# HGRN2 decay-weighted score blocks that grow by a factor of four instead of two

## The chip, the cores and the metric

The kernel runs on one core of one Trainium2 chip. The metric is the device time of one execution in microseconds; the figure for a kernel is the median of its runs. A profile is one further execution, recorded instruction by instruction.

## What is computed

One decoder layer is run for 320 tokens: 256 of one new prompt, and 8 tokens of each of 8 running sequences. An input projection feeds two token mixers, an mLSTM (branch A) and an HGRN2 recurrence (branch B); the branches are projected, gated and merged, and two LayerNorms and a feed-forward block follow. The change lies in branch B. Per head (8 heads, 128 key channels, 256 value channels) it computes

```
G = cumsum(log f)                                   # over the tokens, per channel
a[t,s] = sum_k q[t,k] * exp(G[t,k] - G[s,k]) * (1-f)[s,k]     for s <= t, else 0
o = a @ i + (q * exp(G)) @ S_0
S_new = exp(G_end) * S_0 + ((1-f) * exp(G_end - G))^T @ i
```

Because the decay depends on the channel, `a` isn't one matrix product. It is one product per block pair, once queries carry the decay from their block's start and keys the decay to their block's end.

## The kernel before

**The stream of weights.** All large products have weights as the stationary operand and the 320 tokens as the moving one. There are 304 tiles of 128 output channels; each has 16 contraction steps, and each step three matmuls of 320 columns (high part by high part, high by low, low by high: `bank<-xh,wh`, `xl,wh`, `xh,wl` and the like in the profile), so 304 x 16 x 3 = 14,592 matmuls, in `run_main`. Half a tile is a **unit**: 1,024 weights per partition, 24 matmuls. A unit's weights are fetched by SyncE into one of three buffers `wr`, split by ScalarE (`wh`, line 321) and VectorE (`wl = wr - wh`, line 469, in `prep`) into one of three pairs of buffers, and the pair is free again when its unit's matmuls are done.

**Side work.** Everything else (evacuations, the mixers) is written as Python generators, "chains", that a planner (`Sched`, `pump`) merges into the stream when the program is built. The planner holds a modelled clock for each engine and puts a side operation in when its inputs should be ready by that clock; a TensorE side operation is placed only when its inputs are at least 0.45 us old by the model. What it yields is a fixed order on each of the in-order queues of PE, DVE, ACT, POOL and SP; at run time only semaphores hold an instruction. Side matmuls on f32 data are recorded as two matmul records each.

**Branch B's chains.** A head has six tiles in the stream (two gate tiles, `hf`, `hq` and two of `hi`). From `hf` come the forget gates `fs[:,1]` and the keys `qk[:,0]`; `qk[:,1]` are the queries; `fs[:,0]` starts at one. `h_scan` (VectorE) then goes through block sizes B = 1, 2, 4, ..., 64 (`LEVELS`) and 128. At each size it

- writes `y` (line 1274): in one operation, left halves of each pair of blocks become keys times decay to the block's end, right halves queries times decay from the block's start;
- joins the blocks to blocks of 2B: the left half of `fs[:,0]` is multiplied by the right block's total (line 1279), the right half of `fs[:,1]` by the left one's (line 1281).

`h_a` follows it. For each size from 2 to 64 and each of the three 128-token tiles (two from size 8 on, where the 8-token sequences need no more) TensorE multiplies the tile of `y` as stationary operand with that tile's 64 right-half columns (`self.mm` in line 327), and VectorE copies what belongs to the block pairs into the score matrix `at` under a mask (line 1325). That is 2 x 3 + 4 x 2 = 14 products of 64 columns in a head. Size 1 goes by element products and a sum over channels with ones as weights; size 128 is one product of 128 columns. `y` for sizes from 2 up lies in a pool `yb` of two buffers. `h_state`, `h_i`, `h_out` and `h_sp` take it from there; they don't change.

Of the kernel before, what the change touches and what calls it, by code (L numbers as in the profile page):

```python
# [26 lines left out]
ALPHA = 2.0 ** 0.25  # L27
LEVELS = (1, 2, 4, 8, 16, 32, 64)

# [43 lines left out]

C_ID, C_TRI, C_BM, C_SEL, C_SC, C_END = 0, 128, 256, 320, 328, 968


def constants():
    c = np.zeros((128, C_END), np.float32)
    i = np.arange(128)
    c[:, C_ID:C_ID + 128] = i[:, None] == i[None, :]  # L80
    c[:, C_TRI:C_TRI + 128] = i[:, None] <= i[None, :]

    s = np.arange(64)
    t = s.reshape(2, 4, 8).transpose(1, 0, 2).reshape(64)
    c[64:, C_BM:C_BM + 64] = (s[:, None] <= t[None, :]) & (s[:, None] // 8 == t[None, :] // 8)
    for r in range(4):
        c[r, C_SEL + r] = c[r + 8, C_SEL + r] = 1.0
        c[r + 4, C_SEL + 4 + r] = c[r + 12, C_SEL + 4 + r] = 1.0
    start = np.zeros(TOK, bool)
    start[0] = True  # L90
    start[NP_::NT] = True
    c[:4, C_SC:C_SC + TOK] = ~start
    c[:4, C_SC + TOK:C_SC + 2 * TOK] = np.where(start, -1e38, 0.0)
    m = np.zeros((128, len(LEVELS), 64), np.int32)
    for n, b in enumerate(LEVELS):
        right = (i // b) % 2 == 1
        t = i[right]
        m[:, n, :] = (i[:, None] // (2 * b) == t[None, :] // (2 * b)) & ((i[:, None] // b) % 2 == 0)

    r = np.zeros((2, 64, 2, 4, 4, 8), np.float32)  # L100
    for b in range(NB):
        for n in range(4):
            for i in range(8):
                r[1 - n // 2, 8 * b + i, b // 4, b % 4, n, i] = 1.0
    return c, m.reshape(128, -1), r.reshape(128, 256)

# [120 lines left out]
def acq(pool, n=1):  # L227
    return ("acq", pool, n)
# [55 lines left out]
class Program:  # L284
    def __init__(self, tc, nc, d, pools):
        self.nc, self.d, self.s = nc, d, Sched()
        p, ps, self.dr = pools
        self.cst = p.tile([128, C_END], F32, name="cst")
        self.lmask = p.tile([128, len(LEVELS) * 64], U8, name="lmask")
        self.vec = p.tile([128, V_END], F32, name="vec")  # L290
# [42 lines left out]
    def carve(self):  # L333
# [42 lines left out]
        self.at = Pool([A(512) for _ in range(2)])  # L376
        self.yb = Pool([A(384) for _ in range(2)])
        self.ktk = Pool([A.three(2, 128)])
        self.it2 = [B.three(3, 256) for _ in range(2)]
# [21 lines left out]
    def carve_h(self):  # L401
# [4 lines left out]
        self.pp = Pool([pp])  # L406
        for x in (qz, self.ats0, pp[:, 480:512], *(y[64:128, 2, :] for y in self.it2)):
            self.nc.gpsimd.memset(x, 0.0)
# [180 lines left out]
    def start(self):  # L589
# [21 lines left out]
        self.dma(self.vec, d["vec"])  # L611
        self.dma(self.cst, d["cst"])
        lm = self.f2[:, 0:448].bitcast(I32)
        self.dma(lm, d["lmask"])
        self.dma(self.f2[:, 448:704], d["spread"])
        self.spread = self.ra[:, 6400:6656].rearrange("p (g n) -> p g n", g=2)
        nc.gpsimd.tensor_copy(self.lmask, lm)
        nc.gpsimd.tensor_copy(self.spread, self.f2[:, 448:704].rearrange("p (g n) -> p g n", g=2))
        nc.gpsimd.memset(self.ones_r.bitcast(F32), 1.0)
# [82 lines left out]
    def rows(self, b):  # L702
# [8 lines left out]
        m0 = row(8)  # L711
        emg = row(128)
        sel = self.cst[0:16, C_SEL:C_SEL + 8]
        yield ("sp", 620, lambda: self.dma(m0, self.d["m0"]))
        yield ("pool", 100, lambda: nc.gpsimd.memset(emg, 1.0))
        yield ("act", act(T, True), lambda: self.A(gs, b[0:16, :T]))
# [17 lines left out]
        yield ("dve", dve(T), lambda: v.scalar_tensor_tensor(lf, fx, 0.0, lnu, ALU.min, ALU.subtract))  # L734
        keep = self.cst[0:4, C_SC:C_SC + T]
        low = self.cst[0:4, C_SC + T:C_SC + 2 * T]
        yield ("dve", 2 * dve(T), lambda: v.tensor_tensor_scan(bb, keep, lf, 0.0, ALU.mult, ALU.add))
        yield ("dve", dve(T), lambda: v.tensor_tensor(a, ig, bb, ALU.subtract))
# [445 lines left out]
    def h_start(self, h):  # L1184
# [7 lines left out]
        m["i"] = [Ev(), Ev()]  # L1192
        m["Y"] = [Ev() for _ in range(9)]
        s = self.s
# [58 lines left out]
    def h_scan(self, h):  # L1253

        v, m = self.nc.vector, self.hh[h]
        yield wait(m["f"], m["q"], m["got"])
        qk, fs = m["qk"], m["fs"]
        m["y"] = [None] * 9
        for n, B in enumerate(LEVELS + (128,)):
            T = TOK if B < 8 else NP_  # L1260
            y = yield acq(self.yb if B > 1 else self.pp)
            pat = [[2 * B, T // (2 * B)], [320 + B, 2], [1, B]]
            patq = [[2 * B, T // (2 * B)], [384 + B, 2], [1, B]]
            if B == 1:

                yield ("dve", dve(T), lambda: v.tensor_tensor(y[:, 0:T], qk[:, 0, 0:T], qk[:, 1, 0:T], ALU.mult))
                yo, odd = y[:, T:T + T // 2], lambda x: x[:, 1, 1:T:2]
                yield ("dve", dve(T / 2), lambda: v.tensor_tensor(yo, qk[:, 0, 0:T:2], odd(qk), ALU.mult))
                yield ("dve", dve(T / 2), lambda: v.tensor_tensor(yo, yo, odd(fs), ALU.mult))
            else:  # L1270
                if B < 8:
                    yield ("pool", 150, lambda: self.nc.gpsimd.memset(y[:, 320:384], 0.0))
                yo = y[:, 0:T].rearrange("p (j c i) -> p j c i", c=2, i=B)
                yield ("dve", dve(T), lambda: v.tensor_tensor(yo, cap(qk, 0, patq), cap(fs, 0, pat), ALU.mult))
            m["y"][n] = y
            yield post(m["Y"][n])
            half = lambda x, r: cap(fs, 320 * x + B * r, [[2 * B, T // (2 * B)], [1, B]])
            tot = lambda r: cap(fs, 320 + B * r + B - 1, [[2 * B, T // (2 * B)], [0, B]])
            yield ("dve", dve(T / 2), lambda: v.tensor_tensor(half(0, 0), half(0, 0), tot(1), ALU.mult))
            if B < 128:  # L1280
                yield ("dve", dve(T / 2), lambda: v.tensor_tensor(half(1, 1), half(1, 1), tot(0), ALU.mult))
            if B == 4:
                yield post(m["pre8"])
            if B == 128:

                yield post(m["suf"])

    def h_a(self, h):
# [10 lines left out]
        idb = self.ident.unsqueeze(1).to_broadcast([128, 3, 128])  # L1299
        for n, B in enumerate(LEVELS):  # L1300
            yield wait(m["Y"][n])
            y = m["y"][n]
            w = 3 if B < 8 else 2
            if B == 1:
                hl = yield acq(self.phl)
                yield ("act", act(512), lambda: self.A(hl[0], y))
                yield ("dve", dve(512), lambda: v.tensor_tensor(hl[1], y, hl[0].bitcast(F32), ALU.subtract))
                yield rel(self.pp, y)
            b = yield acq(self.sbank)
            bv = b[:, 0:64 * w]  # L1310
            if B == 1:
                yield ("pe", 2 * pe_r(512), lambda: [self.mm(b, self.ones_r, x, start=i == 0, stop=i == 1) for i, x in enumerate(hl)])
                yield rel(self.phl, hl)
                yield ("dve", dve(384, True), lambda: v.tensor_tensor(a3, b[:, 0:384].rearrange("p (a t) -> p a t", a=3), idb, ALU.mult))
                bv = b[:, TOK:TOK + 192]
            else:
                for i in range(w):
                    c = slice(128 * i, 128 * i + 128)
                    right = y[:, c].rearrange("p (j c i) -> p j c i", c=2, i=B)[:, :, 1, :]
                    yield ("pe", pe_f(64), lambda: self.mm(b[:, 64 * i:64 * i + 64], y[:, c], right, start=True, stop=True))  # L1320
                yield rel(self.yb, y)
            ar = a3[:, 0:w, :].rearrange("p a (j c i) -> p a j c i", c=2, i=B)[:, :, :, 1, :]
            mk = self.lmask[:, 64 * n:64 * n + 64].unsqueeze(1).to_broadcast([128, w, 64]).rearrange("p a (j i) -> p a j i", i=B)
            bv = bv.rearrange("p (a j i) -> p a j i", a=w, i=B)
            yield ("dve", dve(64 * w, True) + (150 if w > 2 else 0), lambda: v.copy_predicated(ar, mk, bv))
            yield rel(self.sbank, b)
        yield wait(m["Y"][7])
        y = m["y"][7]
        b = yield acq(self.sbank)
# [517 lines left out]
    xT=(128, KT, TOK), wif=(128, KT, 8), wt=(len(UNITS), 128, 1024), vec=(128, V_END), m0=(MH, NB), n0=(128, 64),  # L1847
    C0=(MH, NB, 128, 1024), S0=(HH, 128, NB, HV), cst=(128, C_END), lmask=(128, len(LEVELS) * 64), spread=(128, 256),
)
# [70 lines left out]
```

## Time and profile before

| | us |
|---|---|
| median of 3 runs | 2336.71 (2336.39 to 2338.29) |
| the profiled execution | 2337.24 |
| its span, first to last instruction | 2335.5 |
| TensorE (PE) busy | 2320.3 |
| VectorE (DVE) busy | 1370.3 |
| ScalarE (ACT) busy | 1049.6 |
| GpSimd (POOL) busy | 13.4 |

The profile's page gives busy times of each engine, the span in 40 slices, the chain of work that ended last, and groups of instructions by line with the mean length of one. Lengths of TensorE records overlap: a matmul's record lasts until its last result is out, while the next one has long started, so that what a matmul costs the stream is read from the distances between starts. The timeline view lists instructions by their start, and joins neighbours of one kind into a row with their count (`x2`); an f32 product appears as such a row. The waits views tell what an engine's idle time ended with.

### The profile page before, as it was taken

Reading aid. Unit: us, or ns where it says so; the run is one execution under the profiler, and the core shown is the slowest. Engines: PE = TensorE matmul, PEld = TensorE weight load, DVE = VectorE, ACT = ScalarE, POOL = GpSimd, SP = SyncE. Lnnn points to the kernel's source line nnn. Section 1 sums busy time; section 2 is a strip of 40 time slices with the busy share of each in tenths; the row PEclk is TensorE's granted clock in tenths of the full one; section 3 lists DMA queues with packets and bytes.
Section 4 is the critical chain, followed back from the end, with each engine's and each line's share of the span. In section 5 each row is a group of like instructions: output and inputs, shape, how many; then the busy total and the mean of one; then the engine's idle time right before and its main releaser. Section 6 shows DMA issues by size and latency. Waiting matters only on the chain.

```text
span 2335.5 us, 39111 instructions
## 1 busy us (share of the span) xinstructions
PE 2320.3 (99%) x15858; PEld 2274.2 (97%) x15858; DVE 1370.3 (59%) x2320; ACT 1049.6 (45%) x1669; POOL 13.4 (1%) x57
## 2 busy tenths in 40 slices
PE   8999999999999999999999999999999999999998
PEld 7999999999999999999999999999999999999998
DVE  5566557666766776555555767544554455445555
ACT  4444445455555465444433446532443344334434
POOL 0000000000000000000000000000000000000000
PEclk9999999999999999999999999999999999999999
DMA  5777776555555554554555644444444444444465
GB/s 207 258 269 265 256 237 227 196 183 181 181 181 175 183 195 166 181 173 170 176 171 176 221 167 142 147 153 145 149 149 151 148 147 152 150 148 146 153 226 180
DMA packets 143564, 425.03 MB, mean 182 GB/s; under 512 B 16404, under 2 KB 37780, under 8 KB 142360
## 3 DMA queue, kind: packets, MB, share of 16 engines
q1 hardware_dynamic: 142232, 416.25, 51.7%
q0 software_dynamic: 1152, 6.29, 0.8%
q8 instruction: 124, 2.03, 0.4%
q14 instruction: 56, 0.46, 0.1%
HBM read 371.57 MB, written 50.90 MB: 181 GB/s over the span
## 4 chain that ended last, share of the span: by engine, by line
PE 98%; DVE 1%; DMA 0%; ACT 0%; SPq 0%; issue 0%; DVEq 0%
PE bank L327 97%; DVE f3m L1809 0%; DVE f3m L1814 0%; DMA wr<-wt 0%; PE bank L1113 0%; PE bank L1518 0%; PE bank L887 0%; DMA f<-scr 0%; PE bank L1348 0%; SPq L330 0%; PE bank L960 0%; PE bank L1406 0%; PE bank L1353 0%; PE bank L1467 0%; PE bank L934 0%
## 5 line engine op out<-in xcount | busy, mean ns | idle before, releaser
L469 DVE TENSOR_TENSOR wl<-wr,wh 128x1024 fp32r<-128x1024 f32 (+1 forms) x430 | 525.8, 1223 | 474.2 <-ACT wh L321 468.7
L327 PE MATMUL bank<-xh,wh 128*128 128x320 f32 (+1 forms) x2432 | 793.2, 326 | 0.7 <-ACT wh L321 0.7
L327 PE MATMUL bank<-xh,wl 128*128 128x320 f32 (+1 forms) x2432 | 754.0, 310 | 0.0
L327 PE MATMUL bank<-xl,wh 128*128 128x320 f32 (+1 forms) x2432 | 752.0, 309 | 0.0
L321 ACT ACTIVATE wh<-wr 128x1024 fp32r<-128x1024 f32 (+1 forms) x430 | 453.6, 1055 | 448.0 <-PE bank L327 426.1
L327 PEld LDWEIGHTS bank<-xh,wh 128*128 128x128 f32 x2432 | 459.0, 189 | 21.1 <-issue 15.0
L327 PEld LDWEIGHTS bank<-xl,wh 128*128 128x128 f32 x2432 | 459.6, 189 | 3.7
L327 PEld LDWEIGHTS bank<-xh,wl 128*128 128x128 f32 x2432 | 458.4, 188 | 0.2 <-DVE wl L469 0.2
L469 DVE TENSOR_TENSOR bb<-wr,bb 128x1024 fp32r<-128x1024 f32 x179 | 219.3, 1225 | 234.6 <-ACT bb L321 234.5
L327 PE MATMUL bank<-xh,bb 128*128 128x322 f32 x1280 | 287.2, 311 | 0.0
L327 PE MATMUL bank<-ra,bb 128*128 128x320 f32 x1264 | 283.6, 309 | 0.0
L321 ACT ACTIVATE bb<-wr 128x1024 fp32r<-128x1024 f32 x179 | 188.8, 1055 | 207.5 <-PE bank L327 199.8
L327 PE MATMUL bank<-rxb,bb 128*128 128x320 f32 x1112 | 255.4, 309 | 0.0
L327 PE MATMUL bank<-ra,wh 128*128 128x320 f32 x892 | 249.9, 309 | 0.0
L327 PEld LDWEIGHTS bank<-xh,bb 128*128 128x128 f32 x1280 | 215.9, 188 | 0.0
L327 PEld LDWEIGHTS bank<-ra,bb 128*128 128x128 f32 x1264 | 210.7, 188 | 0.4
L327 PE MATMUL bank<-xl,bb 128*128 128x322 f32 x640 | 198.7, 310 | 0.0
L327 PEld LDWEIGHTS bank<-rxb,bb 128*128 128x128 f32 x1112 | 188.4, 188 | 0.2
L321 ACT ACTIVATE f<-f,misc 128x320 f32<-128x320 f32 x210 | 118.2, 563 | 149.5 <-DVE f L1777 137.1
L327 PE MATMUL bank<-rxb,wh 128*128 128x320 f32 x596 | 184.2, 309 | 0.0
L327 PE MATMUL bank<-rxb,wl 128*128 128x320 f32 x596 | 183.8, 308 | 0.0
L327 PEld LDWEIGHTS bank<-ra,wh 128*128 128x128 f32 x892 | 161.5, 188 | 1.1 <-DVE ra L1548 0.9
(257 smaller groups left out, 2230.6 us busy)
## 6 DMA issues: line engine op xcount, KB each, us to landing
wr<-wt SPq DMA_DIRECT2D x607, 512.0 KB, 3.3
rx<-C SPq DMA_DIRECT2D x34, 256.0 KB, 5.7
Cs<-rx SPq DMA_DIRECT2D x34, 256.0 KB, 5.0
f<-C SPq DMA_DIRECT2D x30, 256.0 KB, 4.9
Cs<-f SPq DMA_DIRECT2D x30, 256.0 KB, 4.2
vD<-ra SPq DMA_DIRECT2D x4, 1024.0 KB, 7.1
f<-S SPq DMA_DIRECT2D x8, 512.0 KB, 6.1
f3h<-S SPq DMA_DIRECT2D x8, 512.0 KB, 5.7
```

Source lines behind the costliest of these rows:

```text
L321: return self.nc.scalar.activation(out, in_, func, **kw)
L327: self.nc.tensor.matmul(*a, **kw)
L469: self.V().tensor_tensor(lo[:, c], raw[:, c], hi[:, c].bitcast(F32), ALU.subtract)
```

## The change

Sizes now grow by four: after size 1 come 2, 8 and 32 (`QUADS`), and 128 as before. At each of these sizes four neighbouring blocks are handled together.

- `h_scan` writes into one buffer of 1,024 columns per partition: the keys of all tokens (columns 0 to 319), and from column 384 on, for each group of four blocks, the six (query block, distance) sets: blocks 1, 2, 3 at distance one, 2 and 3 at distance two, 3 at distance three. This takes four VectorE operations (T, 0.75 T, 0.5 T and 0.25 T columns, T being 320 or 256) where two sizes took two of T columns. The two joins to 2B and 4B follow one another. Size 128 is written by two operations of 128 columns.
- `h_a` multiplies each tile's keys once with all its query sets: 192 columns (96 for the third tile, of which half is used), 3 + 2 + 2 = 7 products in a head. Three masked copies per size, one per distance, take the results to `at`: nine in a head beside that of size 1, where there were six.
- `yb` has one buffer instead of two. The buffer of `ktk` moves to the space of `f3h`. The zeros behind the third tile's tokens are set once, and not by GpSimd for each size.
- Nine masks and that of size 1 take 928 columns instead of 448. To make room, `cst` keeps 328 of its 968 columns; the two rows of 320 that the mLSTM's scans read are fetched by two small DMAs into scratch in `rows`.

The diff, without the declarations of sizes:

```diff
-LEVELS = (1, 2, 4, 8, 16, 32, 64)
+QUADS = (2, 8, 32)
+C_KEPT = C_SC
+N_MASK = 64 + 480 + 2 * 192
...
-        self.yb = Pool([A(384) for _ in range(2)])
-        self.ktk = Pool([A.three(2, 128)])
+        self.yb0 = A(1024)
+        self.yb = Pool([self.yb0])
...
+        self.ktk = Pool([C.three(2, 128)])
-        for x in (qz, self.ats0, pp[:, 480:512], *(y[64:128, 2, :] for y in self.it2)):
+        for x in (qz, self.ats0, pp[:, 480:512], self.yb0[:, 320:384], *(y[64:128, 2, :] for y in self.it2)):
...
-        self.dma(self.cst, d["cst"])
-        lm = self.f2[:, 0:448].bitcast(I32)
+        self.dma(self.cst, d["cst"][:, 0:C_KEPT])
+        lm = self.f2[:, 0:N_MASK].bitcast(I32)
...
+        for n, x in enumerate((keep, low)):
+            sc = yield ("sp", 620, lambda: self.dma(x, self.d["cst"][0:4, C_SC + T * n:C_SC + T * n + T]))
...
-        yield ("dve", 2 * dve(T), lambda: v.tensor_tensor_scan(bb, keep, lf, 0.0, ALU.mult, ALU.add))
+        yield ("dve", 2 * dve(T), lambda: v.tensor_tensor_scan(bb, keep, lf, 0.0, ALU.mult, ALU.add), (sc + 3000.0,))
...
+        for n, B in enumerate(QUADS):
+            T = TOK if B == 2 else NP_
+            J = T // (4 * B)
+            z = y = m["y"][n + 1] = yield acq(self.yb)
+            q = lambda o, k: cap(z, 384 + B * o, [[6 * B, J], [B, k], [1, B]])
+            f = lambda o, k: cap(fs, 320 + B * o + B - 1, [[4 * B, J], [B, k], [0, B]])
+            yield ("dve", dve(T), lambda: v.tensor_tensor(z[:, 0:T], qk[:, 0, 0:T], fs[:, 0, 0:T], ALU.mult))
+            run = lambda x, o: cap(x, o + B, [[4 * B, J], [1, 3 * B]])
+            yield ("dve", dve(0.75 * T), lambda: v.tensor_tensor(cap(z, 384, [[6 * B, J], [1, 3 * B]]), run(qk, 384), run(fs, 320), ALU.mult))
+            yield ("dve", dve(T / 2), lambda: v.tensor_tensor(q(3, 2), q(1, 2), f(1, 2), ALU.mult))
+            yield ("dve", dve(T / 4), lambda: v.tensor_tensor(q(5, 1), q(4, 1), f(1, 1), ALU.mult))
+            yield post(m["Y"][n + 1])
+            yield from join(B, T)
+            yield from join(2 * B, T)
...
-                for i in range(w):
-                    c = slice(128 * i, 128 * i + 128)
-                    right = y[:, c].rearrange("p (j c i) -> p j c i", c=2, i=B)[:, :, 1, :]
-                    yield ("pe", pe_f(64), lambda: self.mm(b[:, 64 * i:64 * i + 64], y[:, c], right, start=True, stop=True))
+            for i in range(w):
+                k = 192 if i < 2 else 96
+                yield ("pe", pe_f(k), lambda: self.mm(b[:, 192 * i:192 * i + k], y[:, 128 * i:128 * i + 128], y[:, 384 + 192 * i:384 + 192 * i + k], start=True, stop=True))
+            yield rel(self.yb, y)
+            for d in (1, 2, 3):
+                k, o = (4 - d) * B, (0, 3, 5)[d - 1] * B
+                if B == 2:
+                    J, mk = 40, cap(self.lmask, at_mask, [[k, 40], [1, k]])
+                    to, of = cap(at, d * B, [[4 * B, J], [1, k]]), cap(b, o, [[6 * B, J], [1, k]])
+                    at_mask += 40 * k
+                else:
+                    mk = cap(self.lmask, at_mask, [[0, 2], [k, g], [1, k]])
+                    to, of = cap(at, d * B, [[128, 2], [4 * B, g], [1, k]]), cap(b, o, [[192, 2], [6 * B, g], [1, k]])
+                    at_mask += g * k
+                yield ("dve", dve(w * 32 * (4 - d), True), lambda: v.copy_predicated(to, mk, of))
```

More of the change, by code (lines that the diff above doesn't have):

```diff
@@ L93, in constants @@
     c[:4, C_SC + TOK:C_SC + 2 * TOK] = np.where(start, -1e38, 0.0)
[L94 to L98, printed above, removed]
+    t = i[1::2]
+    m = [i[:, None] == t[None, :] - 1]
+    for b in QUADS:
+        t = np.arange(TOK if b == 2 else 128)
+        own = (t // b) % 4
+        for d in (1, 2, 3):
+            u = t[own >= d] % 128
+            m.append((i[:, None] // (4 * b) == u[None, :] // (4 * b)) & ((i[:, None] // b) % 4 == (u[None, :] // b) % 4 - d))
+    m = np.concatenate(m, axis=1).astype(np.int32)
+    assert m.shape[1] == N_MASK
     r = np.zeros((2, 64, 2, 4, 4, 8), np.float32)
@@ L104, in constants @@
                 r[1 - n // 2, 8 * b + i, b // 4, b % 4, n, i] = 1.0
-    return c, m.reshape(128, -1), r.reshape(128, 256)
+    return c, m, r.reshape(128, 256)
 V_MLG, V_HGG, V_G1, V_B1, V_G2, V_B2, V_LB, V_BI, V_BF, V_END = 0, 16, 32, 48, 64, 80, 96, 112, 113, 114
@@ L287, in __init__ @@
         p, ps, self.dr = pools
-        self.cst = p.tile([128, C_END], F32, name="cst")
-        self.lmask = p.tile([128, len(LEVELS) * 64], U8, name="lmask")
+        self.cst = p.tile([128, C_KEPT], F32, name="cst")
+        self.lmask = p.tile([128, N_MASK], U8, name="lmask")
         self.vec = p.tile([128, V_END], F32, name="vec")
@@ L611, in start @@
         self.dma(self.vec, d["vec"])
-        self.dma(self.cst, d["cst"])
-        lm = self.f2[:, 0:448].bitcast(I32)
+        self.dma(self.cst, d["cst"][:, 0:C_KEPT])
+        lm = self.f2[:, 0:N_MASK].bitcast(I32)
         self.dma(lm, d["lmask"])
-        self.dma(self.f2[:, 448:704], d["spread"])
+        self.dma(self.f2[:, N_MASK:N_MASK + 256], d["spread"])
         self.spread = self.ra[:, 6400:6656].rearrange("p (g n) -> p g n", g=2)
         nc.gpsimd.tensor_copy(self.lmask, lm)
-        nc.gpsimd.tensor_copy(self.spread, self.f2[:, 448:704].rearrange("p (g n) -> p g n", g=2))
+        nc.gpsimd.tensor_copy(self.spread, self.f2[:, N_MASK:N_MASK + 256].rearrange("p (g n) -> p g n", g=2))
         nc.gpsimd.memset(self.ones_r.bitcast(F32), 1.0)
@@ L712, in rows @@
         emg = row(128)
+        keep, low = row(), row()
         sel = self.cst[0:16, C_SEL:C_SEL + 8]
         yield ("sp", 620, lambda: self.dma(m0, self.d["m0"]))
+        for n, x in enumerate((keep, low)):
+            sc = yield ("sp", 620, lambda: self.dma(x, self.d["cst"][0:4, C_SC + T * n:C_SC + T * n + T]))
         yield ("pool", 100, lambda: nc.gpsimd.memset(emg, 1.0))
@@ L734, in rows @@
         yield ("dve", dve(T), lambda: v.scalar_tensor_tensor(lf, fx, 0.0, lnu, ALU.min, ALU.subtract))
-        keep = self.cst[0:4, C_SC:C_SC + T]
-        low = self.cst[0:4, C_SC + T:C_SC + 2 * T]
-        yield ("dve", 2 * dve(T), lambda: v.tensor_tensor_scan(bb, keep, lf, 0.0, ALU.mult, ALU.add))
+        yield ("dve", 2 * dve(T), lambda: v.tensor_tensor_scan(bb, keep, lf, 0.0, ALU.mult, ALU.add), (sc + 3000.0,))
         yield ("dve", dve(T), lambda: v.tensor_tensor(a, ig, bb, ALU.subtract))
@@ L1192, in h_start @@
         m["i"] = [Ev(), Ev()]
-        m["Y"] = [Ev() for _ in range(9)]
+        m["Y"] = [Ev() for _ in range(5)]
         s = self.s
@@ L1257, in h_scan @@
         qk, fs = m["qk"], m["fs"]
[L1258 to L1279, printed above, removed]
-            if B < 128:
-                yield ("dve", dve(T / 2), lambda: v.tensor_tensor(half(1, 1), half(1, 1), tot(0), ALU.mult))
-            if B == 4:
-                yield post(m["pre8"])
-            if B == 128:
-                yield post(m["suf"])
@@ new lines, in h_scan, with join @@
+        m["y"] = [None] * 5
+        half = lambda x, r, B, T: cap(fs, 320 * x + B * r, [[2 * B, T // (2 * B)], [1, B]])
+        tot = lambda r, B, T: cap(fs, 320 + B * r + B - 1, [[2 * B, T // (2 * B)], [0, B]])
+        def join(B, T):
+            yield ("dve", dve(T / 2), lambda: v.tensor_tensor(half(0, 0, B, T), half(0, 0, B, T), tot(1, B, T), ALU.mult))
+            if B < 128:
+                yield ("dve", dve(T / 2), lambda: v.tensor_tensor(half(1, 1, B, T), half(1, 1, B, T), tot(0, B, T), ALU.mult))
@@ new lines, in h_scan @@
+        T = TOK
+        y = m["y"][0] = yield acq(self.pp)
+        yield ("dve", dve(T), lambda: v.tensor_tensor(y[:, 0:T], qk[:, 0, 0:T], qk[:, 1, 0:T], ALU.mult))
+        yo, odd = y[:, T:T + T // 2], lambda x: x[:, 1, 1:T:2]
+        yield ("dve", dve(T / 2), lambda: v.tensor_tensor(yo, qk[:, 0, 0:T:2], odd(qk), ALU.mult))
+        yield ("dve", dve(T / 2), lambda: v.tensor_tensor(yo, yo, odd(fs), ALU.mult))
+        yield post(m["Y"][0])
+        yield from join(1, T)
+        for n, B in enumerate(QUADS):
[13 more added lines that the diff above has]
+            if B == 2:
+                yield post(m["pre8"])
@@ L1288, in h_a @@
+        y = m["y"][4] = yield acq(self.yb)
+        for i in range(2):
+            yield ("dve", dve(128), lambda: v.tensor_tensor(y[:, 128 * i:128 * i + 128], qk[:, i, 128 * i:128 * i + 128], fs[:, i, 128 * i:128 * i + 128], ALU.mult))
+        yield post(m["Y"][4])
+        yield from join(128, NP_)
+        yield post(m["suf"])
     def h_a(self, h):
@@ L1299, in h_a @@
         idb = self.ident.unsqueeze(1).to_broadcast([128, 3, 128])
[L1300 to L1308, printed above, removed]
-            b = yield acq(self.sbank)
[L1310 to L1316, printed above, removed]
-                for i in range(w):
-                    c = slice(128 * i, 128 * i + 128)
-                    right = y[:, c].rearrange("p (j c i) -> p j c i", c=2, i=B)[:, :, 1, :]
-                    yield ("pe", pe_f(64), lambda: self.mm(b[:, 64 * i:64 * i + 64], y[:, c], right, start=True, stop=True))
[L1321 to L1325, printed above, removed]
@@ new lines, in h_a @@
+        yield wait(m["Y"][0])
+        y = m["y"][0]
+        hl = yield acq(self.phl)
+        yield ("act", act(512), lambda: self.A(hl[0], y))
+        yield ("dve", dve(512), lambda: v.tensor_tensor(hl[1], y, hl[0].bitcast(F32), ALU.subtract))
+        yield rel(self.pp, y)
+        b = yield acq(self.sbank)
+        yield ("pe", 2 * pe_r(512), lambda: [self.mm(b, self.ones_r, x, start=i == 0, stop=i == 1) for i, x in enumerate(hl)])
+        yield rel(self.phl, hl)
+        yield ("dve", dve(384, True), lambda: v.tensor_tensor(a3, b[:, 0:384].rearrange("p (a t) -> p a t", a=3), idb, ALU.mult))
@@ new lines, in h_a @@
+        mk = self.lmask[:, 0:64].unsqueeze(1).to_broadcast([128, 3, 64])
+        yield ("dve", dve(192, True) + 150, lambda: v.copy_predicated(a3[:, :, 1:128:2], mk, b[:, TOK:TOK + 192].rearrange("p (a t) -> p a t", a=3)))
+        yield rel(self.sbank, b)
+        at_mask = 64
+        for n, B in enumerate(QUADS):
+            yield wait(m["Y"][n + 1])
+            y = m["y"][n + 1]
+            b = yield acq(self.sbank)
+            w, g = (3 if B == 2 else 2), 128 // (4 * B)
+            for i in range(w):
+                k = 192 if i < 2 else 96
+                yield ("pe", pe_f(k), lambda: self.mm(b[:, 192 * i:192 * i + k], y[:, 128 * i:128 * i + 128], y[:, 384 + 192 * i:384 + 192 * i + k], start=True, stop=True))
+            yield rel(self.yb, y)
+            for d in (1, 2, 3):
+                k, o = (4 - d) * B, (0, 3, 5)[d - 1] * B
+                if B == 2:
+                    J, mk = 40, cap(self.lmask, at_mask, [[k, 40], [1, k]])
[6 more added lines that the diff above has]
+                yield ("dve", dve(w * 32 * (4 - d), True), lambda: v.copy_predicated(to, mk, of))
@@ L1326, in h_a @@
             yield rel(self.sbank, b)
-        yield wait(m["Y"][7])
-        y = m["y"][7]
+        yield wait(m["Y"][4])
+        y = m["y"][4]
         b = yield acq(self.sbank)
@@ L1847 @@
     xT=(128, KT, TOK), wif=(128, KT, 8), wt=(len(UNITS), 128, 1024), vec=(128, V_END), m0=(MH, NB), n0=(128, 64),
-    C0=(MH, NB, 128, 1024), S0=(HH, 128, NB, HV), cst=(128, C_END), lmask=(128, len(LEVELS) * 64), spread=(128, 256),
+    C0=(MH, NB, 128, 1024), S0=(HH, 128, NB, HV), cst=(128, C_END), lmask=(128, N_MASK), spread=(128, 256),
 )
```

## The prediction

> **What bounds the kernel now.** I read the page first, for the span and the busy times, then the table of stretches, then the chain of work that ended last.
>
> ```profile
> span 2335.5 us, 39111 instructions
> PE 2320.3 (99%) x15858; PEld 2274.2 (97%) x15858; DVE 1370.3 (59%) x2320; ACT 1049.6 (45%) x1669; POOL 13.4 (1%) x57
> PE 98%; DVE 1%; DMA 0%; ACT 0%; SPq 0%; issue 0%; DVEq 0%
> ```
>
> ```profile
> 0.00:30.00 30.00, 21.97 (x123) 17.32 (x124) 15.19 (x24) 14.29 (x20) 2.98 (x16) 1.00 0.73 262
> 30.00:2300.00 2270.00, 2269.50 (x15592) 2231.87 (x15591) 1336.24 (x2251) 1018.62 (x1615) 9.89 (x40) 1.00 0.52 180
> 2300.00:2336.00 36.00, 28.80 (x148) 25.03 (x147) 18.85 (x46) 16.74 (x34) 0.53 (x1) 0.94 0.68 247
> ```
>
> ```profile
> 440.00:830.00 390.00, 390.00 (x2806) 378.29 (x2804) 275.33 (x675) 201.03 (x404) 4.07 (x23) 1.00 0.53 181
> ```
>
> Behind a stretch stand its length and the busy time of PE, PEld (TensorE's loads of the stationary operand), DVE, ACT and POOL, then the granted clock. Between 30 and 2300 us TensorE is idle for 0.5 us; from 440 to 830 us, where branch B's scores are made, for nothing, at the full clock. A busy record alone wouldn't prove that the array is kept at its pace, since records overlap; the chain does:
>
> ```profile
> 862.57 1448.69 PE bank L327 x9823
> ```
>
> From 863 us on, 9,823 matmuls follow one another at 1448.69 / 9823 = 0.1475 us, nearly all of them the stream's 320-column ones. So TensorE is the bound; what the change takes out of its queue between 440 and 830 us the end gains, unless TensorE has to wait for something new. ScalarE, VectorE and GpSimd are covered as long as it doesn't.
>
> **What a score product costs the stream.** In the timeline of TensorE a row shows the start. I take the start of the last stream matmul ahead of a product and that of the second one behind it, and subtract two steps of the stream, 0.295 us.
>
> ```profile
> 442.89 0.31 PE L327 MATMUL bank<-xh,wl 128*128 128x320 f32 x1
> 443.04 0.33 PE L327 MATMUL bank<-f 128*128 128x64 f32 x2
> 443.18 0.39 PE L327 MATMUL bank<-xh,wh 128*128 128x320 f32 x1
> 443.41 0.30 PE L327 MATMUL bank<-xl,wh 128*128 128x320 f32 x1
> ```
>
> ```profile
> 773.47 0.31 PE L327 MATMUL bank<-xh,wl 128*128 128x320 f32 x1
> 773.62 0.38 PE L327 MATMUL bank<-f 128*128 128x128 f32 x2
> ...
> 773.99 0.30 PE L327 MATMUL bank<-xl,wh 128*128 128x320 f32 x1
> ```
>
> ```profile
> 776.54 0.31 PE L327 MATMUL bank<-xh,wl 128*128 128x320 f32 x1
> 776.69 0.59 PE L327 MATMUL bank<-f,f 128*128 128x256 f32 x2
> ...
> 777.27 0.31 PE L327 MATMUL bank<-xl,wh 128*128 128x320 f32 x1
> ```
>
> ```profile
> 2304.07 0.31 PE L327 MATMUL bank<-rxb,bb 128*128 128x320 f32 x1
> 2304.22 0.70 PE L327 MATMUL bank<-f,ones 128*128 128x320 f32 x2
> ...
> 2304.90 0.31 PE L327 MATMUL bank<-ra,bb 128*128 128x320 f32 x1
> ```
>
> 64 columns cost 0.52 - 0.295 = 0.225 us, 128 columns the same 0.225, 256 columns 0.435, 320 columns 0.535, each to about 0.01. Below 128 columns there is a floor; above it a line, (0.435 - 0.225) / 128 = 1.64 ns for a column (it gives 0.54 at 320, the row 0.535). I read the floor as the price of loading the keys: behind 64 columns the next stream matmul is also late (443.18 to 443.41 is 0.23, not 0.15).
>
> **The sum on TensorE.** Products of 64 columns in the trace:
>
> ```profile
> L327 PE MATMUL bank<-f 128*128 128x64 f32 x240 | 39.6, 246 | 0.0
> ```
>
> These are 120 products of two records; 8 belong to the mLSTM (one form per head and contraction half, 4 x 2), so 112 go, 14 in each of 8 heads.
>
> - Removed: 112 x 0.225 = 25.2 us.
> - Added: per head 6 products of 192 columns and one of 96. The trace has no 192; its ends are the rows of 128 and 256, 0.225 and 0.435, and I take the line between them, 0.225 + 64 x 0.00164 = 0.33, because a third row (320) lies on the same line. 48 x 0.33 = 15.8 us. With the far ends it would be 10.8 or 20.9. 96 columns lie under the floor: 8 x 0.225 = 1.8 us.
> - Net: 25.2 - 15.8 - 1.8 = **7.6 us** less. With the far ends 12.6 or 2.5; an error of 0.01 on each price moves it by about 1.
>
> All other TensorE work has the same count in both instruction orders.
>
> The Trainium skill has a rule that speaks against this: "TensorE: Matmul & The Clock Gate", section "Back-to-back issue gap", gives a warm matmul N/2.4 + 2.5 ns, and "FP8 and Floating Point Precision", section "TensorE Precision Notes", four passes for true f32. Worked out from these pages, an estimate, 64 columns cost 0.117 us, 96 0.17 and 192 0.33, and the change would add 17.2 - 13.1 = 4.1 us. By it 192 agrees with my line, 64 doesn't: the trace has 0.225. The first page says itself that the formula is too low at small N, since the weight load isn't in it. What that rule would do here is rival 3.
>
> **VectorE.** Mean lengths of its operations by form:
>
> ```profile
> L469 DVE TENSOR_TENSOR wl<-wr,wh 128x1024 fp32r<-128x1024 f32 x428 | 524.4, 1225 | 469.8 <-ACT wh L321 464.3 <-DMA rx<-C 2.4 <-DMA Ss<-f3h 1.0
> ...
> L1274 DVE TENSOR_TENSOR f<-f 128x256 f32<-128x256 f32 x30 | 12.6, 420 | 2.0 <-PE bank L327 1.6
> L1325 DVE COPY_PREDICATED f<-lmask,bank 128x192 f32<-128x192 uint8 x24 | 12.3, 512 | 0.6 <-PE bank L327 0.6
> ...
> L1325 DVE COPY_PREDICATED f<-lmask,bank 128x128 f32<-128x128 uint8 x32 | 9.5, 295 | 0.1
> ...
> L1279 DVE TENSOR_TENSOR f<-f 128x128 f32<-128x128 f32 x30 | 8.7, 290 | 0.2
> ...
> L1274 DVE TENSOR_TENSOR f<-f 128x320 f32<-128x320 f32 x12 | 5.9, 491 | 0.0
> L1279 DVE TENSOR_TENSOR f<-f 128x160 f32<-128x160 f32 x18 | 5.8, 322 | 0.1
> ```
>
> An element operation costs about 0.16 us and 1.03 ns for a column. Per head, `y` from size 2 up took 2 x 0.49 + 5 x 0.42 = 3.08 us. It will take at size 2 0.49 + 0.41 (240 columns) + 0.32 + 0.24 (80), at 8 and 32 each 0.42 + 0.36 + 0.29 + 0.22, and 2 x 0.29 for size 128: 1.46 + 2.58 + 0.58 = 4.62 us, **1.5 us more**. The joins stay. The copies of sizes 2 to 64 took 2 x 0.512 + 4 x 0.295 = 2.2 us. The nine new ones are of forms that the trace lacks; I take 0.295 + 1.03 ns a column: at sizes 8 and 32 0.36 + 0.295 + 0.23 each, and at size 2, whose runs are short, the dearer row, 0.512, for each of three: 3.3 us, **1.1 more** (0.4 if short runs cost nothing extra, 2 if those of 240 elements cost twice). So VectorE gets 2.6 us more a head, 21 us in all: 275 of 390 us becomes 296 of 382, 71% to 78%. All of it lies beside the stream. ScalarE has the same operations; GpSimd loses the sixteen 64-column fills.
>
> What waits behind VectorE is `wl`, and for that TensorE:
>
> ```profile
> L327 PEld LDWEIGHTS bank<-xh,wl 128*128 128x128 f32 x2432 | 458.4, 188 | 0.2 <-DVE wl L469 0.2
> ```
>
> ```profile
> L321 ACT ACTIVATE wh<-wr 128x1024 fp32r<-128x1024 f32 (+1 forms) x430 | 453.6, 1055 | 448.0 <-PE bank L327 426.1
> ```
>
> In the whole run TensorE waited 0.2 us for `wl`. ScalarE splits a unit as soon as TensorE frees a pair (its idle time ends with PE). Two units of 24 x 0.1475 = 3.54 us then still lie ahead, so a margin of 7.08 - 1.055 - 1.225 = **4.8 us** is left for whatever stands ahead of `wl` on VectorE. In the built instruction orders the most other work between two `wl` writes in the heads is 12 operations in the changed kernel; by the lengths above 4.7 us, against 4.3 before; over three units the most is 11.7 against 10.1. That comes to the margin and not past it, and it overstates, since operations overlap their neighbours' ends. I cost it at nothing; if the cover fails, see rivals 1 and 2.
>
> **The single buffer.** The first write of a size's `y` now waits until TensorE has read the former one; on VectorE the next copies, evacuations and `wl` queue behind it. In the changed order that write stands just ahead of the first copy of the former size, and the copy has always needed the same products. The row of copies above shows what that costs today: 0.6 us of waiting in 56 copies. So 32 hand-overs cost VectorE little, and TensorE nothing within the margin. In TensorE's order the heads' products end one tile of the stream earlier than before (tile 93.6 against 94.6 of 304), so no later stage gets anything later.
>
> **The start.**
>
> ```profile
> cst<-cst SPq DMA_DIRECT2D x1, 484.0 KB
> ...
> f<-lmask SPq DMA_DIRECT2D x1, 224.0 KB
> ```
>
> ```profile
> L617 POOL CAST lmask<-f 128x448 uint8<-128x448 int32 x1 | 1.0, 1013 | 17.7 <-DMA f<-lmask 17.7
> ```
>
> ```profile
> 22.70 0.37 SPq L330 DMA_DIRECT2D f<-m  x1
> ```
>
> `cst` falls to 164 KB and `lmask` grows to 464, together 80 KB less, behind the stream's first inputs on SP's queue. The cast grows to 1.013 x 928 / 448 = 2.1 us, an estimate; the fills behind it on GpSimd shift by 1.1 us, and the stream reads none of them. Two small DMAs go out in front of a `wr` fetch, about 2 x 0.37 = 0.7 us on SP; three `wr` buffers cover it. The scan that reads them comes some 19 us later:
>
> ```profile
> 42.26 0.81 DVE L737 TENSOR_TENSOR_SCAN f<-cst,f 4x320 f32<-4x320 f32 x1
> ```
>
> I take nothing for all this, with bounds of -0.5 and +1.
>
> **The sum.** The profiled execution took 2337.24 us, its span and 1.74 us around it; 2337.24 - 7.6 = 2329.6. The median of the three runs lies 0.53 lower, at 2336.71, so I forecast 2329.1 for a median.
>
> **The rivals.**
>
> 1. *Bursts eat part of it.* A head's nine copies and fuller `y` pile up at one place, `wl` comes 0.5 us late once a head: 8 x 0.5 = 4 us back, 2333.1. For it: the burst of 4.7 us against a margin of 4.8. Against it: the 22% of VectorE that stay idle, and 0.2 us of such waiting today.
> 2. *Slower: the single buffer stops VectorE.* If VectorE stands at a hand-over as long as it stands at an evacuation for TensorE today,
>
> ```profile
> DVE f L1209 <- PE bank L327: 55.4, 49, 3.6
> ```
>
> (55.4 us in 49 waits, the longest 3.6, so 1.13 us each) on top of a burst of 4.7, `wl` is 1.0 us late. Twice a head that is 16 us: 2329.1 + 16 = 2345.1. It decides against the change from 7.6 / 16 = 0.48 us each. Against it: the 0.6 us in 56 copies.
>
> 3. *Slower: columns alone set the price* (the pages' rule above). From the line of 1.64 ns a column without the floor, 64 columns cost 0.105 and 14 x 64 = 896 columns a head become 1,248: 8 x 352 x 0.00164 = 4.6 us more, 2341.3. The two equal rows of 64 and 128 columns speak against it.
> 4. *It doesn't shorten the stream*: the freed time shows as waiting of TensorE for scores or banks in the planner's order. 2336.7. Against it: no wait of TensorE in the 390 us.
>
> **How the numbers follow.** Forecast 0.80, rival 1 0.09, rival 2 0.05, rival 3 0.02, rival 4 0.04. A measurement of this kernel tells about 0.2%, 4.7 us, from no change; 2333.1 and 2336.7 count as the same. Faster 0.80, same 0.13, slower 0.07. Range: an error of 0.01 in the prices is 1.2 us, start and runs' spread 1 more below: 2327.0; above it reaches to rival 1 at 2333.2. The far ends of the 192-column price (2324.1 and 2334.2) are left out below and nearly in above, as the line through three rows excludes them.
>
> **What would show it.** In the profile after: no wait of TensorE between 440 and 830 us; rows of 192 columns whose distance costs 0.33; PE's whole busy time shorter by 7 to 8 us; VectorE at 77 to 79% there; nobody waiting for `wl`. It would be wrong if PE rows for `wl` or for `f` show idle time, if 192 columns cost over 0.45, or if copies at size 2 take over 0.8 us.

## The result and the profile after

Over eight runs of each kernel the median falls from 2337.95 to 2330.87 us (2329.57 to 2331.94); the ratio of the times is 0.9971, with a 95% interval of 0.9962 to 0.9980. The profiled execution took 2331.78 us, against 2337.24 before. The medians lie 7.1 us apart; the forecast was 7.6 us less and a median of 2329.1.

The page of the changed kernel, then the stretches (length, busy time of PE, PEld, DVE, ACT and POOL, granted clock, DMA):

```profile
span 2329.7 us, 38945 instructions
PE 2314.0 (99%) x15746; PEld 2266.9 (97%) x15746; DVE 1381.1 (59%) x2400; ACT 1048.4 (45%) x1669; POOL 12.7 (1%) x42
```

```profile
30.00:2294.00 2264.00, 2262.96 (x15485) 2224.53 (x15484) 1347.73 (x2333) 1017.42 (x1615) 8.61 (x25) 1.00 0.53 180
...
440.00:822.00 382.00, 382.00 (x2687) 369.66 (x2686) 285.18 (x758) 199.36 (x407) 2.86 (x9) 1.00 0.54 184
```

The bound is where it was. TensorE has 112 records less, and from 440 to 822 us it never stands idle. VectorE is 75% busy there (285.2 of 382), before 71%.

Where the time went is seen by setting the same matmul of the stream side by side in both traces. These are the first matmul of tile 10 and that of tile 108, before and after all branch-B heads; first the kernel before, then the changed one, both from the timeline of TensorE:

```profile
97.52 0.31 PE L327 MATMUL bank<-xh,wh 128*128 128x320 f32 x1
...
919.94 0.30 PE L327 MATMUL bank<-xh,wh 128*128 128x320 f32 x1
```

```profile
97.70 0.31 PE L337 MATMUL bank<-xh,wh 128*128 128x320 f32 x1
...
912.58 0.30 PE L337 MATMUL bank<-xh,wh 128*128 128x320 f32 x1
```

The stretch between them takes 822.42 us before and 814.88 after: **7.54 us less**. A new product in the timeline, and the groups of the new forms:

```profile
639.28 0.31 PE L337 MATMUL bank<-xh,wl 128*128 128x320 f32 x1
639.43 0.49 PE L337 MATMUL bank<-f 128*128 128x192 f32 x2
639.62 0.44 PE L337 MATMUL bank<-xh,wh 128*128 128x320 f32 x1
639.90 0.31 PE L337 MATMUL bank<-xl,wh 128*128 128x320 f32 x1
```

```profile
L337 PE MATMUL bank<-f 128*128 128x192 f32 x96 | 23.4, 325 | 0.0
L337 PE MATMUL bank<-f 128*128 128x96 f32 x16 | 2.9, 260 | 0.0
```

639.90 - 639.28 - 0.295 = 0.325 us for 192 columns, where the line gave 0.33. For all products that stand alone in the stream, in the two traces, the median prices are 0.223 us for 64 columns, 0.224 for 96, 0.222 for 128, 0.326 for 192, 0.434 for 256 and 0.540 for 320. With these the sum is 112 x 0.223 - 48 x 0.326 - 8 x 0.224 = 7.5 us.

The rest of the difference between the two profiled spans (5.8 instead of 7.5) lies elsewhere, chiefly at one place that the change doesn't touch, in the LayerNorm stage. The timelines of TensorE, ScalarE and VectorE in the changed kernel (in brackets, the idle time before an instruction and what ended it):

```profile
1310.12 0.31 PE L337 MATMUL bank<-rxb,wl 128*128 128x320 f32 x1
1311.35 0.81 PE L337 MATMUL bank<-f,ones 128*128 128x320 f32 x2 [0.92 <-DVE f L1678]
```

```profile
1308.57 1.06 ACT L331 ACTIVATE bb<-wr 128x1024 fp32r<-128x1024 f32 x1 [2.34 <-DMA wr<-wt]
```

```profile
1309.67 1.23 DVE L480 TENSOR_TENSOR bb<-wr,bb 128x1024 fp32r<-128x1024 f32 x1 [1.78 <-ACT bb L331]
1310.81 0.48 DVE L1678 TENSOR_TENSOR f<-f,f3m 128x320 f32<-128x320 f32 x1
```

A weight unit landed late, ScalarE's split waited 2.34 us for it, VectorE's half of the split waited for ScalarE's, and behind it in VectorE's order stood the sum that TensorE needed next: 1.2 us. The profile of the kernel before doesn't have it. Runs 3 and 2 below show that it doesn't take the change to make it.

### The profile page after: what moved, and what is told of

It is laid out like the page before. It is cut to its first block, busy times and chain, and to the rows that moved or that the text cites. A ratio compares the mean times of both kernels' runs of the same rounds, so it can differ in the third digit from the quotient of the medians.

```text
span 2329.7 us, 38945 instructions
## 1 busy us (share of the span) xinstructions
PE 2314.0 (99%) x15746; PEld 2266.9 (97%) x15746; DVE 1381.1 (59%) x2400; ACT 1048.4 (45%) x1669; POOL 12.7 (1%) x42
## 4 chain that ended last, share of the span: by engine, by line
PE 97%; DMA 1%; DVE 1%; ACT 0%; issue 0%; SPq 0%; DVEq 0%; ACTq 0%
PE bank L337 96%; DMA wr<-wt 1%; DVE f3m L1844 0%; DVE f3m L1849 0%; PE bank L1553 0%; PE bank L899 0%; PE bank L1125 0%; DVE bb L480 0%; PE bank L1383 0%; ACT bb L331 0%; ACT wh L331 0%; DVE wl L480 0%; SPq L340 0%; PE bank L972 0%; PE bank L1441 0%
```

## The experiments

Times of the kernel before come from the same chip and session as each run; they differ by a few tenths.

**1. The keys loaded for each piece again.** The changed kernel, with its products cut into pieces of 64 columns:

```diff
-                yield ("pe", pe_f(k), lambda: self.mm(b[:, 192 * i:192 * i + k], y[:, 128 * i:128 * i + 128], y[:, 384 + 192 * i:384 + 192 * i + k], start=True, stop=True))
+                for j in range(0, k, 64):
+                    e = min(k, j + 64)
+                    yield ("pe", pe_f(e - j), lambda: self.mm(b[:, 192 * i + j:192 * i + e], y[:, 128 * i:128 * i + 128], y[:, 384 + 192 * i + j:384 + 192 * i + e], start=True, stop=True))
```

> The changed kernel with each tile's 192 query columns (96 in the third tile) multiplied in pieces of at most 64, so that the keys are loaded three times (twice) again; VectorE's work is the changed kernel's. Theory (a product costs the larger of 0.223 us and 1.64 ns a column, because the keys must be loaded): 6 x (3 x 0.223 - 0.326) + (2 x 0.223 - 0.222) = 2.28 us a head, 18.3 us in all, 2331 + 18 = 2349, slower than the kernel before. Rival (columns alone set the price): the columns are the same, 2331. Rival (the gain came from another order of the work or from fewer instructions on VectorE's side): within 3 us of 2331.

Measured: 2350.25 us, ratio to the kernel before 1.0054 (1.0040 to 1.0067), so 19.4 us above the changed kernel. The same two matmuls of the stream:

```profile
96.95 0.31 PE L337 MATMUL bank<-xh,wh 128*128 128x320 f32 x1
...
931.01 0.31 PE L337 MATMUL bank<-xh,wh 128*128 128x320 f32 x1
```

They lie 834.1 us apart, 19.2 more than in the changed kernel. The theory's 18.3 holds; both rivals are out. All other parts of the change were in place, so the gain comes from putting each tile of keys through TensorE once for all its query sets, and without that the change loses 13 us. The run repeats the load of the keys and the matmul together, so it shows a price per product, and not which of the two makes it. The trace fits the load: behind a product's second load, the next two follow 0.11 us apart each, with 64 columns as with 128, and with 192 they follow 0.16 apart.

**2. Twice the columns in the kernel before.**

```diff
-                    right = y[:, c].rearrange("p (j c i) -> p j c i", c=2, i=B)[:, :, 1, :]
-                    yield ("pe", pe_f(64), lambda: self.mm(b[:, 64 * i:64 * i + 64], y[:, c], right, start=True, stop=True))
+                    yield ("pe", pe_f(64), lambda: self.mm(b[:, c], y[:, c], y[:, c], start=True, stop=True))
...
+                bv = b[:, 0:128 * w].rearrange("p (a j c i) -> p a j c i", a=w, c=2, i=B)[:, :, :, 1, :]
```

> The kernel before, with every product of 64 query columns widened to the whole tile's 128 columns, of which the copies still take the same 64. Theory (64 columns lie under the floor of key loading): nothing, 2338. Rival (columns alone set the price): 112 x 64 x 1.64 ns = 11.8 us, 2350.

Measured: 2338.34 us, ratio 1.0004 (0.9995 to 1.0013). 64 further columns in each of 112 products cost nothing that the times can tell; between tiles 10 and 108 the run takes 823.0 us, 0.6 more than the kernel before, where the rival asked for 11.8. The median price of a lone product of 128 columns is 0.223 us. The floor is shown. It reaches down to a single column: the products with one moving column in this trace (`bank<-misc,f`) cost 0.22 us too.

**3. The changed kernel once more.**

> The changed kernel once more, nothing altered. In its first profile TensorE waited 0.9 us once, at 1311 us, for a VectorE sum that stood behind a weight split that waited for its DMA. Theory (DMA landings differ by execution): a second profile has that wait elsewhere, or not at all, its span is 2328 to 2330, and TensorE's saving up to tile 100 is again 7.4 to 7.6 us. Rival (the new order makes it): the same wait at the same place, span 2329.5 or more.

Measured: 2330.86 us, ratio 0.9971 (0.9960 to 0.9982), the span 2329.6, and 7.55 us less between tiles 10 and 108. The wait came again at the same place (0.8 us), which my theory had not expected. But the rival falls too: run 2, whose order of instructions is that of the kernel before, has it as well,

```profile
PE bank L327 <- DVE f L1645: 1.0, 1, 1.0
```

(line 1645 there is the same sum), while runs 5, 6 and 7, whose orders are forms of the changed one, and run 4 don't. So it is a weak place of both orders that some executions meet: four of the nine profiles of the two kernels and of runs 1 to 7, and that of run 9. In those four it costs 1.1 to 1.3 us each. In each of them VectorE's half of a split waits for ScalarE's just ahead of the sum; but that the weights landed late is named by the profile in the first one and in run 1 only. In runs 2 and 3 it puts ScalarE's wait down to an operation of VectorE, `f3m`, that ended just before the split. What makes the split late in some executions stays open.

**4. One buffer in the kernel before.**

```diff
-        self.yb = Pool([A(384) for _ in range(2)])
+        self.yb = Pool([A(384)])
```

> The kernel before with one buffer for the scores' operands instead of two, nothing else. Theory (a hand-over is hidden by the margin of the weight splits): nothing, 2338, no wait of TensorE from 440 to 830 us. Rival (the single buffer stops VectorE and the splits behind it): up to 16 us, 2354, with waits of TensorE for the low parts of the weights.

Measured: 2337.34 us, ratio 1.0000 (0.9991 to 1.0009), and no wait of TensorE in the heads. Yet the trace shows what the second buffer had been good for. From the end of the `y` that a size needs to the start of its first product, the kernel before leaves 2.0 us at the least and 5.5 at the median of 48 cases. With one buffer it is 0.7 and 1.3, because the planner can write the next `y` only when the last one is read. In the changed kernel it is 0.4 and 0.95 (24 cases). One case of each, the kernel before and then the changed one, VectorE's last operand and TensorE's first product:

```profile
440.09 0.48 DVE L1274 TENSOR_TENSOR f<-f 128x320 f32<-128x320 f32 x1
...
446.47 0.33 PE L327 MATMUL bank<-f 128*128 128x64 f32 x2
```

```profile
638.46 0.24 DVE L1301 TENSOR_TENSOR f<-f 128x80 f32<-128x80 f32 x1
...
639.43 0.49 PE L337 MATMUL bank<-f 128*128 128x192 f32 x2
```

446.47 - 440.57 is 5.9 us, 639.43 - 638.70 is 0.7. The lead is used up for the greater part, but in the changed kernel not overdrawn. In run 1 it once was: TensorE waited 0.4 us there for a query set.

**5 and 6. More work for VectorE.** Each of the nine masked copies issued twice, then four times (the repeats write the same again), and the planner counts them:

```diff
-                yield ("dve", dve(w * 32 * (4 - d), True), lambda: v.copy_predicated(to, mk, of))
+                for _ in range(4):
+                    yield ("dve", dve(w * 32 * (4 - d), True), lambda: v.copy_predicated(to, mk, of))
```

> The changed kernel with each of its nine masked copies in a head issued twice (the second writes the same again): VectorE gets some 23 us more between 440 and 822 us, 285 becomes about 308 of 382. Theory (VectorE's work lies within the margin of the weight splits): nothing, 2331, no wait of TensorE there. Rival (bursts already come to the margin): at least one late split a head of 0.5 us or more, 2335 or more.

> The changed kernel with each of the nine masked copies issued four times: some 70 us more on VectorE, 355 of 382 us. Theory: the cover ends here, since a burst grows by about 3 us over the margin of 4.8; TensorE waits for low parts or scores, a few us a head, 2335 to 2360. Rival (only the mean load of VectorE counts, and it is still under 1): nothing, 2331.

Measured: 2331.18 us with two (ratio 0.9973, 0.9963 to 0.9983) and 2330.74 with four (0.9973, 0.9961 to 0.9985). Neither costs anything that can be told. For four copies my expectation missed, in the time and in the load: VectorE was busy for 298 and 321 us from 440 to 822 us, where I had expected 308 and 355. By the built order the most other work between two weight splits grows only from 4.7 to 5.2 us, since the planner, told of the copies, moves a product back when its operands come late: in this run products start up to 14 us after their operands.

**8 and 9. The same work, not counted.** Four, then seven of each copy, the planner counting one:

```diff
-                yield ("dve", dve(w * 32 * (4 - d), True), lambda: v.copy_predicated(to, mk, of))
+                yield ("dve", dve(w * 32 * (4 - d), True), lambda: [v.copy_predicated(to, mk, of) for _ in range(4)])
```

> The changed kernel with each of the nine masked copies issued four times, and the planner counting one: VectorE's work is that of the former run with four copies (some 321 us busy of 382), but the weight splits stand as far behind as in the changed kernel's order, so the most other work between two splits is 7.5 us by the lengths, over three units 19.0, against 5.2 and 12.8 when the planner counts all. Theory (what decides is the burst ahead of a split against its margin): late splits, about 2 us a head, 2340 to 2360, with waits of TensorE. Rival (only the mean load decides): nothing, 2331, as with the counted copies.

> The same with seven of each copy, the planner counting one: the most other work between two splits is 10.7 us, over three units 26.3. Theory: 8 us late a head or more, 2390 or more. Rival (mean load): VectorE comes to 100% of the stretch, a few us late at its end, 2331 to 2345.

Measured: 2398.08 us with four (ratio 1.0262, 1.0245 to 1.0279), 67 us more than run 6 with the same instructions; the one execution with seven took 2488.69 us. The stretch of run 6, then that of run 8, then the four largest of run 8's waits of TensorE (total, times, longest), and one of them in the timeline:

```profile
440.00:822.00 382.00, 382.00 (x2685) 370.20 (x2684) 320.80 (x925) 200.13 (x397) 2.85 (x9) 1.00 0.54 185
```

```profile
440.00:822.00 382.00, 342.31 (x2299) 322.55 (x2298) 304.15 (x836) 170.36 (x344) 2.49 (x8) 0.97 0.47 160
```

```profile
PE bank L1441 <- DVE f L927: 15.7, 8, 2.2
PE bank L337 <- DVE f L1301: 8.8, 7, 1.4
PE bank L337 <- DVE rh L1394: 8.2, 7, 1.7
PE bank L1502 <- DVE f L1499: 6.7, 4, 2.1
```

```profile
448.87 0.59 PE L337 MATMUL bank<-f 128*128 128x192 f32 x2 [1.30 <-DVE f L1301]
```

With 84% of VectorE in use (320.8 of 382) TensorE waits for nothing; in run 8 the same work is drawn out, VectorE comes to 80% (304.2), and TensorE stands idle for 40 us of the stretch. So the mean load doesn't decide; the order does. But the theory was wrong about the place and, by a factor of four, about the size: TensorE does not wait for the low parts of the weights. The splits are still at least 3.0 us early (3.8 in the kernel before, 4.1 in the changed one). It waits for the operands of side products (the query sets of line 1301, the stacked keys of 927, the split values of 1394, the state's keys of 1499). For the query sets this is the very lead that run 4 found to be short; for the others it wasn't measured. Whether a second buffer would have helped run 8 wasn't tried.

**7. One part of the change alone.** Sizes 8 and 32 by fours, 2 and 4 by pairs, in one buffer:

```diff
-QUADS = (2, 8, 32)
+PAIRS = (2, 4)
+QUADS = (8, 32)
...
+        for n, B in enumerate(PAIRS):
+            y = m["y"][n + 1] = yield acq(self.yb)
+            pat = [[2 * B, T // (2 * B)], [320 + B, 2], [1, B]]
+            patq = [[2 * B, T // (2 * B)], [384 + B, 2], [1, B]]
+            yo = y[:, 0:T].rearrange("p (j c i) -> p j c i", c=2, i=B)
+            yield ("dve", dve(T), lambda: v.tensor_tensor(yo, cap(qk, 0, patq), cap(fs, 0, pat), ALU.mult))
+            yield post(m["Y"][n + 1])
+            yield from join(B, T)
...
```

> One part of the change alone: sizes 8 and 32 handled by fours, sizes 2 and 4 by pairs as before, with one buffer. Theory (the gain is the sum of the products' prices): 8 x (6 x 0.223 - 2 x 0.326 - 0.222) = 3.7 us of the 7.5 are given back, 2334.6; up to tile 100 TensorE is 3.8 us ahead of the kernel before. Rival (columns alone set the price): of 14 x 64 columns size 2 and 4 keep 384 instead of 480, so it would be faster than the changed kernel.

Measured: 2333.75 us, ratio 0.9983 (0.9974 to 0.9992), and 818.4 us between tiles 10 and 108, 4.0 less than before and 3.5 more than the changed kernel. The parts add up as their products' prices do.

No experiment pointed to a kernel faster than the changed one.

## Why the prediction was right, point by point

- **The bound.** Right: TensorE keeps the pace of the stream, and what leaves its queue in the heads leaves the time.
- **The price of a product.** Right. The floor up to 128 columns is shown by run 2, that it is paid for each product by run 1, and the line gave 192 columns within 0.005 us. That the floor is the load of the keys was argued in the prediction and is still argued: the loads' distances fit it, but no run here loads without multiplying.
- **The sum, 7.6.** 7.54 us were measured between tiles 10 and 108; 0.2 of them were there before branch B's heads begin, which is no more than executions differ by. The medians' difference of 7.1 lies 0.5 lower; starts differ by up to 1.4 us between executions (run 4 is 1.2 us ahead at tile 10 with nothing changed there), and the late weight unit takes 1.2 in some.
- **VectorE.** The direction was right, the size too high: 285 us in the stretch and not 296, and 10.8 us more in the whole run (1381.1 after 1370.3), not 21. The forms of copies, in the order of the changed kernel's groups:

```profile
L1360 DVE COPY_PREDICATED f<-lmask,bank 128x192 f32<-128x192 uint8 x16 | 5.9, 369 | 0.0
...
L1360 DVE COPY_PREDICATED f<-lmask,bank 128x240 f32<-128x240 uint8 x8 | 4.1, 515 | 0.0
...
L1360 DVE COPY_PREDICATED f<-lmask,bank 128x80 f32<-128x80 uint8 x8 | 2.6, 324 | 0.0
L1360 DVE COPY_PREDICATED f<-lmask,bank 128x160 f32<-128x160 uint8 x8 | 2.6, 322 | 0.0
```

  At size 2 I took 0.512 for each; that holds for 240 elements, but 160 and 80 cost 0.32. For 80 elements, in runs of two, that is dear (64 elements in longer runs: 0.22); for 160, in runs of four, it is the plain price, and for 240, in runs of six, 0.09 above it. The 0.512 itself was a mean over copies of sizes 1, 2 and 4, from 0.35 to 0.60 us long. The bound of 0.4 us a head for short runs that cost nothing extra comes to 0.55 by the prediction's own prices. Also, operations overlap their neighbours' ends, so that lengths add up to more than busy time.
- **The cover.** Right that it holds, but for the wrong quantity, and so in part by luck. I guarded the weight splits, with a margin of 4.8 us that a burst of 4.7 seemed to exhaust. With the change they are always at least 4.1 us early. The margin was worked out with a unit of 3.54 us; in the heads side products lie between, a unit takes 4.2 us (90 units in 382 us), and at the median a split is 6.5 us early in both kernels. What ran short was the lead of the query sets, from 5.5 to 0.95 us at the median, and rival 2's mechanism, late splits behind a stopped VectorE, is not how this order fails: run 8 shows that it fails at the side products.
- **The single buffer.** Right that it costs no time (run 4). That it takes most of the operands' lead was not seen.
- **The start.** The cast took 1.6 us and not 2.1; tile 10 begins 0.18 us later, well within what executions differ by.
- **The rivals.** Rivals 1 and 2 are out in this order, as TensorE waits for nothing in the heads; rivals 3 and 4 are out by runs 2 and 1, and by the absence of waits.

By the Trainium skill's "TensorE: Matmul & The Clock Gate", section "Back-to-back issue gap", a stream's spacing is set by the weight load and the matmul together. The trace fits it: equal prices from 64 to 128 columns, and 1.64 ns a column above.

## What to carry to other kernels

Where TensorE's queue is the bound, price a small side product by what it does to the stream, from start to start, at several widths: in f32 everything up to 128 moving columns cost 0.22 us here, so fewer products with more columns each win as long as the columns they add cost less than the floors they save. To judge whether added work on another engine is covered, look for the shortest lead among all operands that the bound engine's in-order queue will ask for, side products included; the engine's mean load, and the lead of the main stream's operands, said nothing of it. A removed buffer may cost no time and still use up most of a lead.

## What the runs showed that I had not expected

- With the same VectorE instructions, order alone made 67 us: 2330.7 where the planner counted the copies, 2398.1 where it didn't. Part of it is the clock, as told below: 3% of 382 us is some 11 us, an estimate.
- A weight split that comes late 1.3 ms into the run costs 1.1 to 1.3 us in some executions, always at the same LayerNorm sum, with the changed kernel's order and with that of the kernel before.
- When TensorE's queue had gaps in run 8, its granted clock fell to 0.97 in the stretch, in run 9 to 0.88.

```profile
440.00:822.00 382.00, 310.70 (x1910) 290.74 (x1908) 304.37 (x853) 141.24 (x283) 2.12 (x7) 0.88 0.38 132
```
